# Strassen's block products for five of the eleven feature groups of each FFN, taken in turn with the down projections

## Chip, core and metric

One NeuronCore of one Trainium2 chip runs the whole program. The metric is the device time of one execution in microseconds (us). The kernel before takes 2244.43 us (median of three runs, 2243.63 to 2244.71).

## The reference

A causal decoder of two layers, 256 tokens, model width 2048, in float32. Both layers mix the tokens by attention and then run a gated MLP (the FFN). Layer 0 has dilated attention and four heads of attention to a memory of 256 tokens; layer 1 has stick-breaking attention and four memory heads. The change concerns the FFN alone:

```python
def _conv_ffn(h, w_up, w_conv, b_conv, w_down):
    u = h @ w_up                      # [256, 2048] @ [2048, 2 * 5632]
    gate, val = jnp.split(u, 2, axis=-1)
    gp = jnp.pad(gate, ((0, 0), (CONV_WIDTH - 1, 0), (0, 0)))
    acc = b_conv + gp[:, CONV_WIDTH - 1:CONV_WIDTH - 1 + S] * w_conv[CONV_WIDTH - 1]
    for j in range(CONV_WIDTH - 1):
        acc = acc + gp[:, j:j + S] * w_conv[j]
    return (jax.nn.silu(acc) * val) @ w_down      # [256, 5632] @ [5632, 2048]

def _finish_layer(x, heads, w_o, norms, ...):
    x = x + _rmsnorm(heads @ w_o, norms[1])
    f = _conv_ffn(_rmsnorm(x, norms[2]), ...)
    return x + _rmsnorm(f, norms[3])
```

## The kernel before

**Precision.** Every large product is made of float32r parts: each factor is split into an upper part, hi, and a rest, lo, and three of the four part products are summed (hi hi, lo hi, hi lo; `mm3`, L113 to L115). Weights come from HBM a megabyte at a time (`piece`): a load on the SP queue into one of three `raw` buffers, and then, for each half of 128x1024, a cast on ScalarE (L106, tile `whi`) and a subtraction on VectorE (L107, tile `wlo`); `whi` and `wlo` have four buffers each.

**Up projection.** Features are made in tiles of 128 (`ws_tile`). The weights stand in TensorE and h^T moves. For each of 16 k-tiles there is one matmul of 512 columns (hi of the weight against both parts of h^T, L129, the last one L132) and one of 256 (lo of the weight against hi of h^T, L130). One tile takes one megabyte of weights and 16 such pairs. ScalarE copies half of the PSUM bank out (L133) and VectorE adds the other half (L134). Two tiles make a pair (`ws_pair`): a gate pair, then its value pair. The gate pair is multiplied by 1/rms on VectorE (L576), convolved by one ScalarE instruction a tile (L581) and two VectorE instructions a tile (L584), passed through SiLU (L586), multiplied by 1/rms again (L592) and by the value pair (L595), and split into parts (L247 on ScalarE, L248 on VectorE).

**Down projection.** The activations stand and the weights move (`as_chunk`): a piece of 512 rows by 512 columns is 24 matmuls of 512 columns, into one PSUM bank for each of the two token tiles. PSUM has eight banks: four under the tag `g` and four under the tag `s`.

**Order.** `ffn` (L530 on) takes the 5632 features in parts of 4, 4, 4, 4, 4 and 2 pairs of tiles. After each part come its down projections, for four chunks of 512 columns: one piece a chunk for every 512 features. What they give is copied to the running sum `ys` (tag `sh`, SBUF) by ScalarE in the first part (L554) and added by VectorE in the others (L556). The Tile framework derives all waits and gives each engine its own instruction order from modelled costs; small steps of other work are hung at the start of later feature tiles (`later` and `step`). Layer 0's FFN lies at about 384 to 1134 us of the profiled execution, layer 1's at 1499 to 2226 us.

Of the kernel before, what the change touches and what calls it, by code (L numbers as in the profile page):

```python
# [29 lines left out]
# columns of the packed per-feature vectors  # L30
# [3 lines left out]
# FFN parts, in pairs of 128-feature tiles  # L34
PARTS = (4, 4, 4, 4, 4, 2)

# order in which the q and k tiles of mixer A are made: dilated head by head
# [6 lines left out]
class Body:  # L44
    def __init__(self, ctx, tc, a):
        self.tc, self.nc, self.a = tc, tc.nc, a
        self.sb = ctx.enter_context(tc.tile_pool(name="sb", bufs=1))
        self.todo = []
        self.psp = ctx.enter_context(tc.tile_pool(name="ps", bufs=1, space=bass.MemoryType.PSUM))

# [85 lines left out]
    def ws_pair(self, src, h, out=None, before=None, R=None):  # L136
        """Two of them, [P, 2, tok], times R."""
# [44 lines left out]
    def sums(self, n):  # L182
        """Room for the partial means of squares of n token tiles, with eps as the last part."""
# [4 lines left out]
    def rstd(self, ss):  # L188
        """[P, n, 5], the parts of mean(x^2) + eps -> 1 / rms, [P, n]."""
# [11 lines left out]
    def spread(self, r, name):  # L201
        """[P, 2] per token -> [P, 256], the same on every partition."""
# [15 lines left out]
    def scaled_T(self, src, kt, g, h):  # L218
        """h^T of one 128-feature tile, times its gain, in two parts."""
# [53 lines left out]
    def mem_heads(self, qm, mk, mv, outs, first):  # L273
        """Softmax attention to the memory, its steps taken at the coming units from `first` on."""
# [42 lines left out]
    def rotate(self, q, kinds):  # L317
        """Two feature tiles [e, 2, tok]: times 1 / rms and rotated (q also times E^-0.5)."""
# [77 lines left out]
    def sb_pair(self, j, q, k, V, outs, first):  # L396
        """Stick-breaking attention of heads 2j and 2j+1. q, k: [e, 2, tok]."""
# [5 lines left out]
    def sb_scores(self, q, k, st):  # L403
# [14 lines left out]
        # softplus(z), in the form that can't overflow  # L418
# [4 lines left out]
        # sums over this and the later keys  # L423
# [36 lines left out]
    def scaled_chunk(self, src, h, r, before=None, later=None):  # L460
        """[tok, 512] times r; `later`: r comes as late as that unit."""
# [15 lines left out]
    def add_normed(self, ys, r, t, each=None):  # L477
        """x += y g / rms(y) for one token tile; ys: four [tok, 2, 512] chunks that hold y g."""
# [8 lines left out]
    def out_proj(self, layer, src, lhs, each, filler=None):  # L487
# [3 lines left out]
        for c0 in (0, 2):  # L491
# [12 lines left out]
            # the first two chunks side by side: the last heads are needed late  # L504
# [11 lines left out]
            if late:  # L516
                # token tile by token tile: the end of the first one lies behind the second
# [12 lines left out]
    def ffn(self, layer, h, each, filler=None, done=None):  # L530
        nc = self.nc
        up, dn = self.a["up%d" % layer], self.a["dn%d" % layer]
# [6 lines left out]

        def spread():  # L540
# [3 lines left out]

        self.later(1, rms)
# [3 lines left out]
        base = 0  # L549

        def evac(part, c, t, b, gs):
            y = ys[c][:, t, :]
            if part == 0:
                nc.scalar.copy(y, b)  # L554
            else:
                nc.vector.tensor_add(y, y, b)  # L556
            if gs:
# [3 lines left out]
                nc.vector.tensor_tensor(y, y, gs[c], op=ALU.mult)  # L561

        for part, npairs in enumerate(PARTS):
            last = part == len(PARTS) - 1
            acts = []
            for p in range(base, base + npairs):
                if p % 2 == base % 2:
                    ahi = self.sh([P, 4, S], F32R)
                    alo = self.sh([P, 4, S], F32R)
                    o = 0  # L570
                ga = self.ws_pair(up[p, 0], h)
                if p == 0:
                    # 1 / rms of the first pair comes late
                    val = self.ws_pair(up[p, 1], h)
                Rb = spread().unsqueeze(1).to_broadcast([P, 2, S])
                nc.vector.tensor_tensor(ga, ga, Rb, op=ALU.mult)  # L576
                c = self.pairtile()
                for j in range(2):
                    ft = 2 * p + j
                    w = [self.cols[:, cv + i * NFT + ft:cv + i * NFT + ft + 1] for i in range(4)]  # L580
                    nc.scalar.activation(c[:, j, :], ga[:, j, :], AF.Identity, scale=w[2], bias=w[3])  # L581
                    for i in (1, 0):
                        d = 2 - i
                        nc.vector.scalar_tensor_tensor(c[:, j, d:], ga[:, j, :S - d], w[i], c[:, j, d:],  # L584
                                                       op0=ALU.mult, op1=ALU.add)
                nc.scalar.activation(c, c, AF.Silu)  # L586
                if layer == 0 and p == NFT // 2 - 1:
                    # one table set serves Exp and Ln in what follows
                    tc = self.tc
                    tc.keep_in_program_order(  # L590
                        nc.scalar.preload_act_table_set("natural_log_exp_and_others"))
                nc.vector.tensor_tensor(c, c, Rb, op=ALU.mult)  # L592
                if p:
                    val = self.ws_pair(up[p, 1], h)
                nc.vector.tensor_tensor(c, c, val, op=ALU.mult)  # L595
                self.split_heads(c, ahi[:, o:o + 2, :], alo[:, o:o + 2, :])
                acts += [(ahi[:, o + j, :], alo[:, o + j, :]) for j in range(2)]
                o += 2
# [261 lines left out]
```

## Time and profile before

| | |
|---|---|
| runs, median (lowest to highest) | 2244.43 us (2243.63 to 2244.71) |
| span of the profiled execution | 2242.5 us |
| TensorE (PE) busy | 2227.6 us, 99% |
| VectorE (DVE) busy | 1451.5 us, 65% |
| ScalarE (ACT) busy | 1148.6 us, 51% |
| GpSimd (POOL) busy | 19.0 us, 1% |
| granted TensorE clock, mean | 0.999 of full |
| moved by DMA | 422.39 MB, 188 GB/s |

PE, DVE, ACT, POOL and SP are the five engines. A busy time counts the execution of instructions and not the issue of transfers. A timeline row gives start, duration, engine, line, operation, destination<-sources, shape and count, and in brackets how long the engine had been idle and what ended that. Durations of successive instructions overlap a little, since an engine starts one before the last has drained: so the distance of two starts is the price of a queued instruction, and the duration that of one that stands alone.

### The profile page before, as it was taken

The numbers are of one execution on the slowest core, as the hardware profiler recorded it, in microseconds if no ns is written. First come the engines' busy times: TensorE is split into PE (matmuls) and PEld (weight loads), VectorE is DVE, ScalarE is ACT, GpSimd is POOL, SyncE is SP. The second block draws the span as 40 slices with busy tenths as digits, with TensorE's granted clock in tenths as the row PEclk, the third lists the DMA queues.
The fourth block names the chain that finished last, engine by engine and source line by source line (L and its number), as shares of the span: only waits on it lengthen the run. The fifth ranks groups of instructions, "written<-read, shape, count | busy, mean of one in ns | idle before, by whom it ended". The sixth has DMA issues, their size and how long they took to land.

```text
span 2242.5 us, 28970 instructions
## 1 busy us (share of the span) xinstructions
PE 2227.6 (99%) x11682; PEld 1895.7 (85%) x11682; DVE 1451.5 (65%) x1879; ACT 1148.6 (51%) x1614; POOL 19.0 (1%) x42
## 2 busy tenths in 40 slices
PE   9999999999999999999999999999999999999998
PEld 7888888888888888888888888878888888888886
DVE  6567767756656566665774676567566665666657
ACT  6545656545445454454564545455454454544544
POOL 0000000000000000000000000000000000000000
PEclk9999999999999999999999999999999999999999
DMA  8754555555555555555545445545555555555553
GB/s 309 269 180 160 191 194 182 188 188 188 188 188 188 188 188 188 188 188 189 187 169 188 154 166 179 190 176 188 188 188 188 188 188 188 188 188 188 188 188 131
DMA packets 61607, 422.39 MB, mean 188 GB/s; under 512 B 7073, under 2 KB 7457, under 8 KB 11937
## 3 DMA queue, kind: packets, MB, share of 16 engines
q1 hardware_dynamic: 60192, 416.35, 53.8%
q0 software_dynamic: 1280, 4.20, 0.7%
q8 instruction: 91, 1.49, 0.3%
q14 instruction: 44, 0.35, 0.0%
HBM read 418.42 MB, written 2.10 MB: 188 GB/s over the span
## 4 chain that ended last, share of the span: by engine, by line
PE 98%; issue 1%; DMA 0%; DVE 0%; ACT 0%; SPq 0%; POOLq 0%; POOL 0%; DVEq 0%; ACTq 0%
PE ps_g L129 38%; PE ps_g L130 20%; PE ps_g L113 12%; PE ps_g L115 11%; PE ps_g L114 11%; PE ps_g L132 3%; PE ps_s L234 1%; DMA raw<-in_wmv_dram 0%; PE ps_s L285 0%; PE ps_s L312 0%; PE ps_s L391 0%; PE ps_s L409 0%; PE ps_s L449 0%; PE ps_s L348 0%; PE ps_s L304 0%
## 5 line engine op out<-in xcount | busy, mean ns | idle before, releaser
L129 PE MATMUL ps_g<-h,whi 128*128 128x512 f32 x3600 | 1283.9, 399 | 0.2 <-DVE h L224 0.2
L107 DVE TENSOR_TENSOR wlo<-raw,whi 128x1024 fp32r<-128x1024 f32 (+1 forms) x758 | 924.3, 1221 | 534.6 <-ACT whi L106 531.3
L106 ACT CAST whi<-raw 128x1024 fp32r<-128x1024 f32 (+1 forms) x758 | 794.2, 1048 | 563.2 <-PE ps_g L114 341.2
L130 PE MATMUL ps_g<-h,wlo 128*128 128x256 f32 x3840 | 1038.5, 281 | 0.0
L129 PEld LDWEIGHTS ps_g<-h,whi 128*128 128x128 f32 x3600 | 676.2, 188 | 155.4 <-DVE h L224 0.7
L130 PEld LDWEIGHTS ps_g<-h,wlo 128*128 128x128 f32 x3840 | 724.8, 189 | 22.2
L113 PE MATMUL ps_g<-whi,sh 128*128 128x512 f32 x824 | 325.6, 395 | 0.0
L115 PE MATMUL ps_g<-wlo,sh 128*128 128x512 f32 x824 | 323.1, 392 | 0.0
L114 PE MATMUL ps_g<-whi,sh 128*128 128x512 f32 x824 | 320.4, 389 | 0.0
L133 ACT COPY qk<-ps_g 128x256 f32<-128x256 f32 x224 | 83.6, 373 | 337.5 <-PE ps_g L132 337.5
L134 DVE TENSOR_TENSOR qk<-ps_g,qk 128x256 f32<-128x256 f32 x224 | 95.0, 424 | 163.1 <-ACT qk L133 161.0
L115 PEld LDWEIGHTS ps_g<-wlo,sh 128*128 128x128 f32 x824 | 154.7, 188 | 36.0
L114 PEld LDWEIGHTS ps_g<-whi,sh 128*128 128x128 f32 x824 | 154.7, 188 | 34.4 <-DVE sh L248 0.3
L113 PEld LDWEIGHTS ps_g<-whi,sh 128*128 128x128 f32 x824 | 154.9, 188 | 30.8 <-ACT sh L247 0.2
L113 PE MATMUL ps_g<-whi,h 128*128 128x512 f32 x280 | 110.5, 395 | 2.0 <-ACT whi L106 2.0
L115 PE MATMUL ps_g<-wlo,h 128*128 128x512 f32 x280 | 109.7, 392 | 0.1
L114 PE MATMUL ps_g<-whi,h 128*128 128x512 f32 x280 | 109.6, 392 | 0.0
L132 PE MATMUL ps_g<-h,whi 128*128 128x512 f32 x240 | 95.6, 398 | 0.0
L584 DVE SCALAR_TENSOR_TENSOR qk<-qk,cols 128x254 f32<-128x254 f32 (+1 forms) x176 | 73.1, 478 | 0.0
L556 DVE TENSOR_TENSOR sh<-sh,ps_g 128x512 f32<-128x512 f32 x76 | 51.8, 684 | 21.5 <-PE ps_g L115 21.5
L113 PEld LDWEIGHTS ps_g<-whi,h 128*128 128x128 f32 x280 | 52.5, 188 | 14.5 <-ACT whi L106 3.6
L115 PEld LDWEIGHTS ps_g<-wlo,h 128*128 128x128 f32 x280 | 52.5, 188 | 12.9 <-DVE wlo L107 1.6
(152 smaller groups left out, 1059.7 us busy)
## 6 DMA issues: line engine op xcount, KB each, us to landing
raw<-in_up_dram SPq DMA_DIRECT2D x176, 1024.0 KB, 4.8
raw<-in_dn_dram SPq DMA_DIRECT2D x88, 1024.0 KB, 4.8
raw<-in_wqk_a_dram SPq DMA_DIRECT2D x24, 1024.0 KB, 4.9
raw<-in_wo_b_dram SPq DMA_DIRECT2D x16, 1024.0 KB, 4.9
raw<-in_wv_a_dram SPq DMA_DIRECT2D x12, 1024.0 KB, 4.8
raw<-in_wv_b_dram SPq DMA_DIRECT2D x12, 1024.0 KB, 4.8
raw<-in_wk_b_dram SPq DMA_DIRECT2D x12, 1024.0 KB, 4.8
raw<-in_wq_b_dram SPq DMA_DIRECT2D x12, 1024.0 KB, 4.8
```

The source lines that it names most:

```text
L106: nc.scalar.copy(hi[:, ns], r)
L107: nc.vector.tensor_sub(lo[:, ns], r, hi[:, ns].bitcast(F32))
L113: mm(out, lhi, rhi, start=start, stop=False)
L114: mm(out, llo, rhi, start=False, stop=False)
L115: mm(out, lhi, rlo, start=False, stop=stop)
L129: mm(b, whi[:, ks], both, start=kt == 0, stop=False)
L130: mm(b[:, 0:S], wlo[:, ks], one, start=False, stop=False)
L132: mm(b, whi[:, ks], both, start=False, stop=True)
L133: nc.scalar.copy(out, b[:, S:])
L134: nc.vector.tensor_add(out, b[:, 0:S], out)
L556: nc.vector.tensor_add(y, y, b)
L584: nc.vector.scalar_tensor_tensor(c[:, j, d:], ga[:, j, :S - d], w[i], c[:, j, d:], op0=ALU.mult, op1=ALU.add)
```

## The change

The features of one layer are seen as eleven groups of 512 gate and 512 value features. Groups 0, 2, 4, 6, 8 and 10 ("narrow") are made the old way. Groups 1, 3, 5, 7 and 9 ("wide") are made by a form of Strassen's scheme with seven block products and eight sums of results: token tile against token tile, k-tile against k-tile, gate against value. The new `wide` takes one group in eight units of two k-tiles. A unit is one megabyte of weights in four 128x512 blocks (b11, b21, b22, b12; array `uw`), from which VectorE makes the sums t1 and t3 and, in place, b22 and b21 (L584, L585, L588, L589); blocks and sums are split into parts (L573 on ScalarE, L574 on VectorE). Seven products of three matmuls of 512 columns each (L116 to L118) are summed over the units in seven PSUM banks. h^T stands; its own block sums are made once a layer (`sums_of_h`), in the place that memory's tile `h1` had. The parts `fc` and `fd` of a unit lie in one buffer, `forms`, in the place of the residual stream x, which is sent to DRAM (`xout`) early in the FFN and loaded again ahead of the last narrow group. At the end of a wide group two ScalarE instructions (L607) and eight VectorE ones (L610) make four [128 tokens, 512] tiles of the banks, with 1/rms applied; in `turned`, at the second and third tile of the next narrow group, sixteen PE transposes (L725) turn them, and convolution and product read them from PSUM.

Down projections are no longer taken after parts but in turn with the units: each wide group after a layer's first has eight units and eight down pieces (two groups by four chunks), and the first one has four. A token tile's half of a down piece has its own `s` bank, which ScalarE copies to an `sc` tile (L663; four buffers); an accumulating DMA issued by GpSimd adds that tile to `ys` (L664). There are 144 of these, each of 256 KB from SBUF to SBUF. Group 9's down pieces and group 10's stand at the end and are added as before. Layer 0 also makes the memory's h^T for layer 1 a second time, in its last narrow group (`again`, not shown).

```diff
+    def wide(self, src, h, s, forms, r):
+        ps = {i: self.bank("g" if i in (1, 2, 6, 7) else "s") for i in range(1, 8)}
...
+        for u in range(n):
+            raw = self.sb.tile([P, 2048], F32, name="raw", tag="raw", bufs=3)
+            nc.sync.dma_start(raw, src[u])
+            b11, b21, b22, b12 = (raw[:, i * 512:(i + 1) * 512] for i in range(4))
...
+            nc.vector.tensor_sub(t1, b12, b11)
+            nc.vector.tensor_sub(t3, b22, b12)
+            split(*fa, raw[:, 0:1024])
+            split(*(f[:, 0:512] for f in fb), b22)
+            nc.vector.tensor_sub(b22, b22, t1)
+            nc.vector.tensor_sub(b21, b21, b22)
+            for i, of in enumerate((t1, t3)):
+                split(*(f[:, i * 512:(i + 1) * 512] for f in fc), of)
+            split(*fd, raw[:, 512:1536])
+            product(1, u, *fa, 0)
+            product(2, u, *fa, 1)
+            product(3, u, *fb, 0)
+            yield
+            product(7, u, *fc, 1)
+            product(5, u, *fc, 0)
+            product(6, u, *fd, 1)
+            product(4, u, *fd, 0)
+            if u < n - 1:
+                yield
+        a = [self.sc([P, 512]) for _ in range(2)]
+        g0, v1 = self.sc([P, 512]), self.sc([P, 512])
...
+            nc.scalar.activation(a[t], ps[1], AF.Copy, scale=rt[t])
...
+        add(g0, 2, 0, a[0])
+        add(a[1], 7, 1, a[1])
...
-    def ffn(self, layer, h, each, filler=None, done=None):
+    def ffn(self, layer, h, each, filler=None, done=None, late=None):
...
+                part = self.sc([P, 512])
+                nc.scalar.copy(part, b)
+                nc.gpsimd.dma_start(y, part, accum_op=ALU.add)
+
+        def down(g, c):
+            parts = self.piece(dn[c, g])
+            for t in range(2):
+                b = self.bank("s")
+                self.as_mm([b, b], parts, acts[g], 0, (t,))
+                evac(g, c, t, b)
+                yield
...
+        narrow(0)
+        before, forms = [0], None
+        for g in WIDE:
...
+            w = self.wide(uw[WIDE.index(g)], h, s, forms, R[0])
+            downs = [down(b, c) for b in before for c in range(4)]
+            share = KT // 2 // len(downs)
+            for u in range(KT // 2):
+                d = downs[u // share] if u % share == 0 else iter(())
+                next(d, None)
+                next(w)
+                next(d, None)
+                next(w)
+            for i in range(2):
+                self.later(1 + i, lambda made=self.made, i=i, g=g: turned(g, made, i))
...
+            narrow(g + 1)
+            before = [g + 1, g]
```

In the orders below a row is one instruction: line, operation, destination<-sources with buffer numbers, shape. The first place is VectorE in the midst of an FFN. Before, between two up tiles:

```order
L584 SCALAR_TENSOR_TENSOR qk_5565<-qk_5473,cols_61,qk_5565 128x255 x2
L584 SCALAR_TENSOR_TENSOR qk_5565<-qk_5473,cols_61,qk_5565 128x254 x2
L107 TENSOR_TENSOR wlo_5673<-raw_5670,whi_5672 128x1024
L592 TENSOR_TENSOR qk_5565<-qk_5565,R_3509 128x512
L134 TENSOR_TENSOR qk_5574<-ps_g_5575,qk_5574 128x256
L107 TENSOR_TENSOR wlo_5677<-raw_5670,whi_5676 128x1024
L107 TENSOR_TENSOR wlo_5718<-raw_5715,whi_5717 128x1024
L134 TENSOR_TENSOR qk_5574<-ps_g_5620,qk_5574 128x256
L595 TENSOR_TENSOR qk_5565<-qk_5565,qk_5574 128x512
L107 TENSOR_TENSOR wlo_5722<-raw_5715,whi_5721 128x1024
L248 TENSOR_TENSOR sh_5472<-qk_5565,sh_5471 128x512
```

There the splitting of up weights (`wlo`) alternates with the convolution and with the sum of a tile's two bank halves. After, one unit of a wide group with its down piece:

```order
L584 TENSOR_TENSOR qk_5211<-raw_5209 128x512
L574 TENSOR_TENSOR x_3797<-raw_5124,x_3797 128x1024
L585 TENSOR_TENSOR qk_5212<-raw_5209 128x512
L110 TENSOR_TENSOR wlo_5186<-raw_5183,whi_5185 128x1024
L110 TENSOR_TENSOR wlo_5190<-raw_5183,whi_5189 128x1024
L574 TENSOR_TENSOR wlo_5214<-raw_5209,whi_5213 128x1024
L574 TENSOR_TENSOR wlo_5216<-raw_5209,whi_5215 128x512
L574 TENSOR_TENSOR x_3797<-qk_5212,x_3797 128x512
L588 TENSOR_TENSOR raw_5209<-raw_5209,qk_5211 128x512
L574 TENSOR_TENSOR x_3797<-qk_5211,x_3797 128x512
L589 TENSOR_TENSOR raw_5209<-raw_5209 128x512
```

The t1 of the next unit stands ahead of this unit's last split, and the two splits of the down piece (L110) ahead of the four of the unit's blocks. Nothing there reads PSUM any more.

The second place is PE between two up tiles. Before, the tile `ps_g_5866` ends and the next begins:

```order
L129 MATMUL ps_g_5866<-h2_2651,whi_5873 128x512
L130 MATMUL ps_g_5866<-h2_2651,wlo_5874 128x256
L129 MATMUL ps_g_5866<-h2_2651,whi_5873 128x512
L130 MATMUL ps_g_5866<-h2_2651,wlo_5874 128x256
L129 MATMUL ps_g_5866<-h2_2651,whi_5873 128x512
L130 MATMUL ps_g_5866<-h2_2651,wlo_5874 128x256 x2
L132 MATMUL ps_g_5866<-h2_2651,whi_5873 128x512
L129 MATMUL ps_g_5911<-h2_2651,whi_5914 128x512
L130 MATMUL ps_g_5911<-h2_2651,wlo_5915 128x256
L129 MATMUL ps_g_5911<-h2_2651,whi_5914 128x512
L130 MATMUL ps_g_5911<-h2_2651,wlo_5915 128x256
L129 MATMUL ps_g_5911<-h2_2651,whi_5914 128x512
```

After, the first up tile that follows a wide group, and what stands behind it:

```order
L132 MATMUL ps_g_5453<-h2_2654,whi_5460 128x512
L133 MATMUL ps_g_5453<-h2_2654,wlo_5461 128x256 x2
L135 MATMUL ps_g_5453<-h2_2654,whi_5460 128x512
L725 MATMUL ps_s_5499<-ident_65,sc_5440 128x128
L725 MATMUL ps_s_5499<-ident_65,sc_5439 128x128
L725 MATMUL ps_s_5499<-ident_65,sc_5440 128x128
L725 MATMUL ps_s_5499<-ident_65,sc_5439 128x128
L725 MATMUL ps_s_5504<-ident_65,sc_5438 128x128
L725 MATMUL ps_s_5504<-ident_65,sc_5441 128x128
L725 MATMUL ps_s_5504<-ident_65,sc_5438 128x128
L725 MATMUL ps_s_5504<-ident_65,sc_5441 128x128
L132 MATMUL ps_g_5498<-h2_2654,whi_5524 128x512
```

Eight transposes of the wide group's results (`sc`) stand between the first and the second up tile.

The third place is VectorE at the down projections' end. Before, the sums of down results, between splits:

```order
L107 TENSOR_TENSOR wlo_5404<-raw_5401,whi_5403 128x1024
L107 TENSOR_TENSOR wlo_5408<-raw_5401,whi_5407 128x1024
L556 TENSOR_TENSOR sh_3296<-sh_3296,ps_g_5327 128x512
L107 TENSOR_TENSOR wlo_5438<-raw_5435,whi_5437 128x1024
L556 TENSOR_TENSOR sh_3296<-sh_3296,ps_g_5328 128x512
L107 TENSOR_TENSOR wlo_5442<-raw_5435,whi_5441 128x1024
L107 TENSOR_TENSOR wlo_5478<-raw_5475,whi_5477 128x1024
L107 TENSOR_TENSOR wlo_5482<-raw_5475,whi_5481 128x1024
L556 TENSOR_TENSOR sh_3297<-sh_3297,ps_g_5399 128x512
L107 TENSOR_TENSOR wlo_5523<-raw_5520,whi_5522 128x1024
L556 TENSOR_TENSOR sh_3297<-sh_3297,ps_g_5400 128x512
```

After, the end of a wide group; the results of the down pieces have gone to the accumulating DMA, and the rows with `sc` are the eight sums of products:

```order
L110 TENSOR_TENSOR wlo_5525<-raw_5522,whi_5524 128x1024
L110 TENSOR_TENSOR wlo_5529<-raw_5522,whi_5528 128x1024
L610 SCALAR_TENSOR_TENSOR sc_5440<-ps_g_4778,small_3389,sc_5438 128x512
L610 SCALAR_TENSOR_TENSOR sc_5439<-ps_g_4783,small_3389,sc_5439 128x512
L610 SCALAR_TENSOR_TENSOR sc_5438<-ps_g_4782,small_3389,sc_5438 128x512
L610 SCALAR_TENSOR_TENSOR sc_5439<-ps_g_4782,small_3389,sc_5439 128x512
L610 SCALAR_TENSOR_TENSOR sc_5441<-ps_s_4781,small_3389,sc_5439 128x512
L610 SCALAR_TENSOR_TENSOR sc_5438<-ps_s_4781,small_3389,sc_5438 128x512
L610 SCALAR_TENSOR_TENSOR sc_5439<-ps_s_4780,small_3389,sc_5439 128x512
L610 SCALAR_TENSOR_TENSOR sc_5438<-ps_s_4779,small_3389,sc_5438 128x512
L110 TENSOR_TENSOR wlo_5602<-raw_5599,whi_5601 128x1024
L137 TENSOR_TENSOR qk_5452<-ps_g_5453,qk_5452 128x256
```

The eight sums stand behind four splits of up weights, of which the last two are shown; the PE rows above read their results.

More of the change, by code (lines that the diff above doesn't have):

```diff
@@ L538, in rms @@
             R.append(rx)
+            for t in range(2):
+                nc.sync.dma_start(self.xout[t], self.x[:, t, :])
         def spread():
@@ L543, in spread @@
             return R[1]
+        s, make = self.sums_of_h(h)
+        for i in range(KT // 2):
+            self.later(i, lambda i=i: make(i))
         self.later(1, rms)
@@ L561, in evac @@
                 nc.vector.tensor_tensor(y, y, gs[c], op=ALU.mult)
[L563 to L571, printed above, removed]
+            else:
+                part = self.sc([P, 512])
+                nc.scalar.copy(part, b)
+                nc.gpsimd.dma_start(y, part, accum_op=ALU.add)
@@ new lines, in ffn @@
+        for c in range(4):
+            g = WIDE[-1]
+            b = self.as_chunk(dn[c, g:], acts[g])
+            for t in range(2):
+                evac(g, c, t, b[t])
+        g = GROUPS - 1
+        gs = [self.gain(2 * layer + 1, c) for c in range(4)]
+        if not filler:
+            banks = [[self.bank(), self.bank()] for _ in range(2)]
+            banks += [[self.bank("s"), self.bank("s")] for _ in range(2)]
+            store = self.stores("h1") + self.stores("h2")
+            parts = [self.piece(dn[c, g], store=store[c]) for c in range(4)]
+            for t in range(2):
+                for c in range(4):
+                    self.as_mm(banks[c], parts[c], acts[g], 0, (t,))
+                    evac(g, c, t, banks[c][t], gs)
+                self.add_normed(ys, r[t], t, lambda c: done(t, c))
+            return
@@ L617, in ffn @@
+        for c in range(4):
+            b = self.as_chunk(dn[c, g:], acts[g])
+            for t in range(2):
+                evac(g, c, t, b[t], gs)
         self.add_normed(ys, r[0], 0)
```

161 lines of the change are left out of this document (115 added, 46 removed).

## The prediction

> **What bounds the kernel now.** I read the page's shares first, then its chain of waits, then one window inside layer 0's FFN.
>
> ```profile
> span 2242.5 us, 28970 instructions
> ...
> PE 2227.6 (99%) x11682; PEld 1895.7 (85%) x11682; DVE 1451.5 (65%) x1879; ACT 1148.6 (51%) x1614; POOL 19.0 (1%) x42
> ...
> PE 98%; issue 1%; DMA 0%; DVE 0%; ACT 0%; SPq 0%; POOLq 0%; POOL 0%; DVEq 0%; ACTq 0%
> ```
>
> The chain that ends last is TensorE for 98% of the span. The other engines and the transfers are covered, so only fewer or shorter matmuls shorten this kernel, as long as the cover lasts. How much cover there is stands in the windows (PE, PEld, DVE, ACT, POOL busy with counts, clock, share of the DMA engines, GB/s):
>
> ```profile
> 510.00:600.00 90.00, 90.00 (x508) 78.01 (x507) 59.76 (x77) 47.53 (x64) 0.00 (x0) 1.00 0.55 187
> ```
>
> VectorE has a third of its time free here, ScalarE half, the DMA engines 45%. At the granted clock of 1.00 the matmul paces come from two timelines. VectorE's, inside the up projections:
>
> ```profile
> 547.62 0.69 DVE L576 TENSOR_TENSOR qk<-qk,R 128x512 f32<-128x512 f32 x1
> 548.23 1.22 DVE L107 TENSOR_TENSOR wlo<-raw,whi 128x1024 fp32r<-128x1024 f32 x1
> 549.36 1.66 DVE L584 SCALAR_TENSOR_TENSOR qk<-qk,cols 128x255 f32<-128x255 f32 x4
> 550.94 1.22 DVE L107 TENSOR_TENSOR wlo<-raw,whi 128x1024 fp32r<-128x1024 f32 x1
> 552.07 0.69 DVE L592 TENSOR_TENSOR qk<-qk,R 128x512 f32<-128x512 f32 x1
> ...
> 558.46 0.42 DVE L134 TENSOR_TENSOR qk<-ps_g,qk 128x256 f32<-128x256 f32 x1 [1.05 <-ACT qk L133]
> 558.92 0.69 DVE L595 TENSOR_TENSOR qk<-qk 128x512 f32<-128x512 f32 x1
> 559.53 1.22 DVE L107 TENSOR_TENSOR wlo<-raw,whi 128x1024 fp32r<-128x1024 f32 x1
> 560.67 0.68 DVE L248 TENSOR_TENSOR sh<-qk,sh 128x512 fp32r<-128x512 f32 x1
> ...
> 569.77 0.42 DVE L134 TENSOR_TENSOR qk<-ps_g,qk 128x256 f32<-128x256 f32 x1 [1.01 <-ACT qk L133]
> ```
>
> L134 ends a feature tile. From 558.46 to 569.77 two tiles pass, so a tile costs (569.77 - 558.46) / 2 = 5.655 us of TensorE. The same rows price VectorE. Standing in a queue, a 128x1024 takes 560.67 - 559.53 = 1.14 us and a 128x512 takes 559.53 - 558.92 = 0.61; alone they take 1.22 and 0.69. TensorE's timeline in a down projection (L113 to L115 in turn):
>
> ```profile
> 497.62 0.39 PE L113 MATMUL ps_g<-whi,sh 128*128 128x512 f32 x1
> ...
> 501.05 0.39 PE L113 MATMUL ps_g<-whi,sh 128*128 128x512 f32 x1
> ```
>
> Fifteen matmuls lie between these two starts: 3.43 / 15 = 0.2288 us each, so a down piece of 24 costs 5.49.
>
> **TensorE's gain.** A group of 512 + 512 features is eight tiles: 8 x 5.655 = 45.2 us go. A wide group puts in their place 8 units x 7 products x 3 = 168 matmuls of the down projections' kind, 168 x 0.2288 = 38.4, and 16 transposes. Those are priced by a row of the chain:
>
> ```profile
> 368.87 1.75 PE ps_s L234 x16
> ```
>
> 16 cost 1.75 us. The net is 45.2 - 38.4 - 1.75 = 5.05 us a group, and 50.5 us for ten groups. All the rest of the sum is what the shorter cover lets through. The rows for that, groups of one form (count, busy, mean ns) and the transfers (median us from issue to landing):
>
> ```profile
> L107 DVE TENSOR_TENSOR wlo<-raw,whi 128x1024 fp32r<-128x1024 f32 x754 | 921.5, 1224 | 533.6 <-ACT whi L106 530.4 <-PE ps_s L234 1.6
> L106 ACT CAST whi<-raw 128x1024 fp32r<-128x1024 f32 x754 | 791.8, 1051 | 562.2 <-PE ps_g L114 341.2 <-PE ps_g L129 148.0 <-issue 59.3
> L224 DVE SCALAR_TENSOR_TENSOR h<-sh,cols,h 128x256 fp32r<-128x256 f32 x48 | 20.4, 481 | 5.4 <-ACT h L223 5.4
> L247 ACT CAST sh<-qk 128x512 fp32r<-128x512 f32 x44 | 27.4, 622 | 12.0 <-DVE qk L595 12.0
> L554 ACT COPY sh<-ps_g 128x512 f32<-128x512 f32 x16 | 9.3, 582 | 15.3 <-PE ps_g L115 15.3
> L483 DVE SCALAR_TENSOR_TENSOR x<-sh,small,x 128x512 f32<-128x512 f32 x32 | 22.3, 750 | 1.2 <-POOL small L194 0.9
> L474 POOL DMA_DIRECT2D sc<-in_gb_dram x16 | 9.0, 560 | 559.3 <-DVE sc L440 252.3 <-DVE qk L134 199.1 <-DVE sh L500 68.2
> ```
>
> ```profile
> raw<-in_up_dram SPq DMA_DIRECT2D x176, 1024.0 KB, 4.8
> ...
> sc<-in_gb_dram POOLq DMA_DIRECT2D x16, 256.0 KB, 4.5
> ...
> x<-in_x_dram SPq DMA_DIRECT2D x2, 1024.0 KB, 6.8
> ```
>
> **A unit with its down piece.** TensorE needs 21 + 24 matmuls, 45 x 0.2288 = 10.30 us. VectorE needs seven 128x512 (t1, t3, b22, b21, fb, two halves of fc) and two 128x1024 (fa, fd), 7 x 0.61 + 2 x 1.14 = 6.55, and 2.28 for the piece: 8.83 queued, 7 x 0.69 + 4 x 1.22 = 9.7 alone. Both lie under 10.30, but only by 15 and 6%. ScalarE has four casts of 1024, three of 512 and two bank copies, 4 x 1.05 + 3 x 0.62 + 2 x 0.58 = 7.2. TensorE still leads. An order of these instructions walked by hand with those durations has VectorE finish each form 4 to 5 us before TensorE wants it, and each `s` bank is copied out 1.3 us before its next use: no stall from these.
>
> **Loads.** By VectorE's order a unit's load can start when the second split of a piece (L110) has freed a `raw` buffer; it must have landed for that unit's t1; and behind t1 come the last unit's fd, t3 and the next piece's two splits, 2 x 0.61 + 3 x 1.14 = 4.64, with 0.08 for the last to drain. So a loop of load, sums, splits and release closes in L + 4.72 us, L being a load's landing. It costs TensorE nothing while that is under 10.3 us, L under 5.6; beyond, 8 x (L - 5.58) builds up over a group, of which the 4.4 us of VectorE's lead are free. L was 4.8 with the loads evenly spaced. In the new order a piece's load and a unit's start 3.7 us apart, so the second shares the engines with the first for 4.8 - 3.7 = 1.1 us, and the 0.5 MB of accumulation add to it. From the window: 90 us at 0.55 and 187 GB/s move 16.8 MB, so a megabyte takes 3.1 us of all 16 engines and 256 KB takes 0.77. Half of a 0.77 lands on such a load: L = 4.8 + 1.1 + 0.35 = 6.25. That is 8 x 0.67 - 4.4 = 1.0 us a group, 8 us for the eight groups of this kind. The ends are 0 (L = 4.8) and, with the x loads' 6.8, 5.4 a group.
>
> **End of a wide group.** The eight sums wait for four splits of up weights, and the fifth (into `v1`) waits for an `sc` buffer that the last accumulating DMA must have read and released. That tile is copied out 4.3 us after the last units' start (S); with the 4.5 us of the 256 KB row, `v1` starts at about S + 9 and the sums that follow take three times 0.7. TensorE meets the first transposes behind one tile, at S + 5.5 + 5.65 = S + 11.15. So the stall is 0 to 1.8; I take 1.0, times eight: 8 us. Behind it wait up tiles on TensorE and their splits on VectorE. Each microsecond by which the accumulation lands later is a microsecond here. The Trainium skill's page DMA: Bandwidth & Descriptors (Anatomy of one DMA — SWDGE (gpsimd) path) gives about 2.0 us plus bytes / 436 GB/s for a transfer issued by GpSimd, an estimated 2.6 us here; by it the 8 us would vanish, but the row of this trace has 4.5, and the sum goes by the row.
>
> **The first wide group of a layer** has four pieces for eight units: TensorE 8 x 4.80 + 4 x 5.49 = 60.4 us, VectorE 8 x 6.55 + 4 x 2.28 = 61.5. VectorE is the bound there, and its splits start up to 4.1 us behind the end of group 0, since the last product and split of that group stand ahead of them: 1.1 + 4.1 = 5.2 a layer, 10.4 in all. With durations taken alone VectorE would have 8 x 7.27 + 4 x 2.44 = 68.
>
> **The narrow groups.** VectorE has 16 splits, eight L134, conv and products, and the turned halves: about 42 us queued, 47.5 alone, against 8 x 5.655 + 1.75 = 47.0. No stall, or 0.5. In group 0 no sums of products or turned halves stand, but eight makings of h^T's block sums do: 2 x 0.61 and four of 128 elements, each at most the 0.42 of an L134, so 1.2 to 2.9 us; at 2.0 that group needs 45 against 45.2, and I take 1 us a layer. The memory's h^T made again is 16 x 0.48 = 8 us of VectorE in the last narrow group, for which I take 2, and 0.5 a layer for a later start of the FFN: 5 in all. x to DRAM and back hides under 700 us. The 144 accumulations keep GpSimd at 144 x 0.56 = 81 us of a span of 2242; it has nothing else.
>
> **The sum:** -50.5 + 8 + 8 + 10.4 + 5 = -19.1. From the span 2242.5 - 19.1 = 2223.4; the median lies 1.9 above the span, so 2225.
>
> **Rivals.**
> All covers hold: loads stay near 4.8 and the accumulation lands sooner than VectorE gets to `v1`. What is left is half of the first groups' 10.4 and the 5: -50.5 + 10 = -40, 2204. For it speak the free shares in the window, against it that the first group has no cover left on VectorE.
>
> VectorE takes over, with instructions that cost what they cost alone, since most of the new ones wait for a cast: first groups 2 x (68 - 60.4 + 4.1) = 23, ends 8 x 1.8 = 14, narrow groups 8 x 0.5 = 4 and group 0 2 x 3 = 6, the memory 3: +50, and nothing is gained, 2244. For it speaks that VectorE stood 530 us idle before L107 for L106; against it that L106 itself stood idle for TensorE (341 and 148 us), which frees the buffers, and not for its own speed.
>
> Slower: the accumulating DMAs fill the 16 engines. Each reads its tile, and reads and writes `ys`. At 6.8 us a load, as for x beside other loads, a group loses 5.4 us, 43 for eight: -50.5 + 43 + 23.4 = +16, 2261; at 7.0 it would be 2274. The point from which the change loses is L = 6.54, only 0.3 above what I take. For it speaks the short margin; against it that the bytes rise by a tenth and the engines are at 0.55. The Trainium skill's page DMA: Bandwidth & Descriptors (Issuing engines are not separate DMA queues) says that transfers of all issuing engines run on the same 16 engines and interleave; by that the loads do pay for the accumulation, which is this rival. The 6.8 agrees with it.
>
> That the change doesn't do what it says I leave at nothing: the order has 1680 matmuls of 512 more and 1280 pairs fewer.
>
> **How the numbers follow.** A measurement tells about 0.2%, 4.5 us, from no change. My sum has 0.48, the covers 0.17, VectorE 0.14, the accumulation 0.21. Of the first a little reaches into the zone of no change, and a little of VectorE's out of it. Faster 0.64, same 0.14, slower 0.22. The range goes from 2206, just above where all covers hold, to 2258, just under the slower rival's 2261; alone, my own case would have 2212 to 2238.
>
> **What would show it.** In the profile after: TensorE's share down from 99% by the stalls (about 31 us of idle time), PE waits on `sc` at L725 of about 1 us, on the forms at L116 in the first wide group of each layer, the megabyte of `uw` landing in about 6.3 us. I am wrong if those loads land under 5.5 (then it is faster) or over 6.5, if VectorE's 512-wide rows stand at 0.69 apart, or if the transposes wait more than 2 us.

## The result and the profile after

The changed kernel takes 2327.75 us (median of four runs, 2317.21 to 2337.0) against 2244.03: the ratio is 1.037, 95% interval 1.035 to 1.039. It is slower by 84 us where 19 less were forecast, and outside the range.

The page of the changed kernel, with its transfers (section 6: KB each, median us from issue to landing):

```profile
span 2329.3 us, 29420 instructions
...
PE 2221.3 (95%) x10962; PEld 1845.9 (79%) x10962; DVE 1760.9 (76%) x2447; ACT 1328.2 (57%) x1970; POOL 142.0 (6%) x186
...
q0 software_dynamic: 22016, 41.95, 9.9%
...
PE 48%; issue 41%; POOL 5%; DVE 3%; DMA 2%; ACT 1%; SPq 0%; POOLq 0%; DVEq 0%; ACTq 0%
...
raw<-in_uw_dram SPq DMA_DIRECT2D x80, 1024.0 KB, 6.7
sh<-sc POOLq DMA_DIRECT2D x144, 256.0 KB, 7.0
```

Of the 144 accumulating DMAs 128 stand in the wide groups with eight pieces, 16 in each, and the other 16 carry group 9's down pieces at the layers' ends; only group 10's are added as before.

TensorE has 720 matmuls fewer and 108 us without work, where before it had 15. The chain doesn't tell why: 41% of it is "issue", time that it puts down to nothing. So I read stages. In TensorE's records a wide group with eight pieces runs from its first L116 to the first L132 behind it: the eight of them took 88.6 to 92.5 us, mean 91.0, against 82.4 of matmuls. The narrow group behind it took 52.3 to 54.5 us against 47.0 (without the one that also makes the memory's h^T). The same two stages in windows (columns as in the prediction), one wide group and the narrow one behind it:

```profile
681.00:773.00 92.00, 85.91 (x364) 68.23 (x362) 71.75 (x89) 54.84 (x75) 13.48 (x16) 0.98 0.76 217
773.00:828.00 55.00, 49.88 (x276) 43.07 (x274) 41.29 (x61) 26.89 (x41) 0.10 (x1) 0.94 0.53 176
```

VectorE is busy for 72 of 92 us: it isn't the bound, though TensorE waits. The DMA engines went from 0.55 to 0.76. What was waited for (us in total, times, longest), over the whole span:

```profile
DVE qk L584 <- DMA raw<-in_uw_dram: 119.1, 49, 4.0
...
PE ps_s L116 <- ACT sc L663: 46.3, 42, 2.1
DVE sc L610 <- issue: 42.2, 15, 4.3
...
PE ps_s L725 <- DVE sc L610: 35.5, 8, 5.1
```

There are two stalls. **In the wide group** VectorE's t1 (L584) waits for the unit's load, and TensorE waits for ScalarE's copy of an `s` bank (L663). The queue of SP and VectorE's timeline show how they hang together:

```profile
714.92 0.33 SPq L578 DMA_DIRECT2D raw<-in_uw_dram  x1
...
725.89 0.33 SPq L578 DMA_DIRECT2D raw<-in_uw_dram  x1
...
738.70 0.33 SPq L578 DMA_DIRECT2D raw<-in_uw_dram  x1
...
749.86 0.33 SPq L578 DMA_DIRECT2D raw<-in_uw_dram  x1
```

```profile
712.54 2.36 DVE L110 TENSOR_TENSOR wlo<-raw,whi 128x1024 fp32r<-128x1024 f32 x2
...
722.30 0.69 DVE L584 TENSOR_TENSOR qk<-raw 128x512 f32<-128x512 f32 x1 [0.84 <-DMA raw<-in_uw_dram]
...
723.51 2.36 DVE L110 TENSOR_TENSOR wlo<-raw,whi 128x1024 fp32r<-128x1024 f32 x2
...
733.98 0.69 DVE L584 TENSOR_TENSOR qk<-raw 128x512 f32<-128x512 f32 x1 [3.97 <-DMA raw<-in_uw_dram]
```

A piece's second split ends at 712.54 + 2.36 = 714.90, and the load starts at 714.92; t1 starts at 722.30, 7.4 us later; the next two splits end at 725.87, and the next load starts at 725.89. It is the loop of the prediction, closing in 11.0, 12.8 and 11.2 us where TensorE needs 10.30. From t1 to the release of the buffer it takes 4.7 us, as predicted, or 3.6, as from 722.30, where fd's split has gone ahead of t1.

How this reaches TensorE is in ScalarE's row order. The cast of fd waits for VectorE's L589, the copy of the `s` bank stands behind that cast, and TensorE waits for the copy:

```profile
719.16 1.04 ACT L573 CAST x<-raw 128x1024 fp32r<-128x1024 f32 x1 [5.82 <-DVE raw L589]
720.11 0.58 ACT L663 COPY sc<-ps_s 128x512 f32<-128x512 f32 x1
```

```profile
720.74 0.50 PE L116 MATMUL ps_s<-whi,sh 128*128 128x512 f32 x1 [2.03 <-ACT sc L663]
```

**Behind the wide group** TensorE's timeline shows the first transposes:

```profile
778.83 0.27 PE L725 MATMUL ps_s<-ident,sc 128*128 128x128 f32 x1
784.23 1.77 PE L725 MATMUL ps_s<-ident,sc 128*128 128x128 f32 x7 [5.12 <-DVE sc L610]
```

and VectorE's and GpSimd's the reason:

```profile
775.09 2.73 DVE L610 SCALAR_TENSOR_TENSOR sc<-ps_g,small,sc 128x512 f32<-128x512 f32 x4 [1.94 <-issue]
782.10 2.73 DVE L610 SCALAR_TENSOR_TENSOR sc<-ps_s,small,sc 128x512 f32<-128x512 f32 x4 [4.28 <-issue]
```

```profile
767.83 0.85 POOL L664 DMA_DIRECT2D sh<-sc  x1 [7.07 <-ACT sc L663]
772.26 0.84 POOL L664 DMA_DIRECT2D sh<-sc  x1 [3.58 <-ACT sc L663]
```

The first four sums start 7.3 us after the last accumulating DMA but one was issued, the second four (`v1` first) 9.8 us after the last one. That one landed just before them. The transfers issued between 772.0 and 772.5 are this one:

```profile
sh<-sc POOLq DMA_DIRECT2D x1, 256.0 KB, 9.8
```

In all eight groups the last one took 8.5 to 9.8 us to land, and the second four sums started within 0.1 us of it. The wait itself bears no name, "issue"; that it is the `sc` buffers had to be tested.

### The profile page after: what moved, and what is told of

It reads as the page before. It is cut to its first block, busy times and chain, and to the rows that moved or that the text cites. A ratio compares the mean times of both kernels' runs of the same rounds, so it can differ in the third digit from the quotient of the medians.

```text
span 2329.3 us, 29420 instructions
## 1 busy us (share of the span) xinstructions
PE 2221.3 (95%) x10962; PEld 1845.9 (79%) x10962; DVE 1760.9 (76%) x2447; ACT 1328.2 (57%) x1970; POOL 142.0 (6%) x186
## 4 chain that ended last, share of the span: by engine, by line
PE 48%; issue 41%; POOL 5%; DVE 3%; DMA 2%; ACT 1%; SPq 0%; POOLq 0%; DVEq 0%; ACTq 0%
PE ps_g L132 16%; PE ps_g L133 9%; PE ps_g L116 5%; PE ps_g L118 5%; PE ps_g L117 5%; POOL sh L664 4%; PE ps_g L135 1%; PE ps_s L116 1%; PE ps_s L118 1%; PE ps_s L117 1%; DMA sh<-sc 1%; DVE wlo L110 1%; PE ps_s L237 1%; DMA sc<-in_gb_dram 0%; DVE x L574 0%
## 5 line engine op out<-in xcount | busy, mean ns | idle before, releaser
L110 DVE TENSOR_TENSOR wlo<-raw,whi 128x1024 fp32r<-128x1024 f32 (+1 forms) x598 | 720.4, 1219 | 225.9 <-ACT whi L109 222.3
L132 PE MATMUL ps_g<-h,whi 128*128 128x512 f32 x2400 | 868.6, 403 | 0.9 <-ACT whi L109 0.7
L133 PE MATMUL ps_g<-h,wlo 128*128 128x256 f32 x2560 | 696.7, 282 | 1.6 <-DVE wlo L110 1.6
L132 PEld LDWEIGHTS ps_g<-h,whi 128*128 128x128 f32 x2400 | 456.9, 190 | 107.1 <-ACT sc L607 1.8
L133 PEld LDWEIGHTS ps_g<-h,wlo 128*128 128x128 f32 x2560 | 489.0, 191 | 15.2 <-DVE wlo L110 2.8
L116 PE MATMUL ps_s<-whi,sh 128*128 128x512 f32 x576 | 232.9, 405 | 46.7 <-ACT sc L663 46.3
L573 ACT CAST x<-raw 128x1024 fp32r<-128x1024 f32 x80 | 83.9, 1049 | 260.5 <-DVE raw L589 207.4
L118 PE MATMUL ps_s<-wlo,sh 128*128 128x512 f32 x576 | 228.7, 397 | 0.0
L117 PE MATMUL ps_s<-whi,sh 128*128 128x512 f32 x576 | 227.4, 395 | 1.0 <-DVE sh L251 1.0
L664 POOL DMA_DIRECT2D sh<-sc x144 | 122.5, 851 | 1372.5 <-ACT sc L663 1358.8
L116 PEld LDWEIGHTS ps_s<-whi,sh 128*128 128x128 f32 x576 | 109.4, 190 | 90.2 <-ACT sc L663 67.0
L116 PE MATMUL ps_g<-whi,h 128*128 128x512 f32 x440 | 172.7, 392 | 1.9 <-ACT whi L109 1.8
L117 PE MATMUL ps_g<-whi,h 128*128 128x512 f32 x440 | 172.3, 392 | 0.0
L118 PE MATMUL ps_g<-wlo,h 128*128 128x512 f32 x440 | 171.0, 393 | 0.1
L136 ACT COPY qk<-ps_g 128x256 f32<-128x256 f32 x144 | 53.5, 371 | 177.0 <-PE ps_g L135 176.8
L573 ACT CAST whi<-raw 128x1024 fp32r<-128x1024 f32 (+1 forms) x160 | 131.0, 836 | 40.0 <-DMA raw<-in_uw_dram 15.4
L574 DVE TENSOR_TENSOR wlo<-raw,whi 128x1024 fp32r<-128x1024 f32 (+1 forms) x160 | 146.8, 956 | 0.0
L584 DVE TENSOR_TENSOR qk<-raw 128x512 f32<-128x512 f32 x80 | 55.4, 693 | 119.1 <-DMA raw<-in_uw_dram 119.1
L117 PEld LDWEIGHTS ps_s<-whi,sh 128*128 128x128 f32 x576 | 109.3, 190 | 25.7 <-DVE sh L251 3.0
L118 PEld LDWEIGHTS ps_s<-wlo,sh 128*128 128x128 f32 x576 | 109.3, 190 | 24.5
L574 DVE TENSOR_TENSOR x<-raw,x 128x1024 fp32r<-128x1024 f32 x80 | 97.9, 1224 | 30.6 <-ACT x L573 30.5
```

The lines of the kernel that those rows point to most:

```text
L110: nc.vector.tensor_sub(lo[:, ns], r, hi[:, ns].bitcast(F32))
L116: mm(out, lhi, rhi, start=start, stop=False)
L117: mm(out, llo, rhi, start=False, stop=False)
L118: mm(out, lhi, rlo, start=False, stop=stop)
L132: mm(b, whi[:, ks], both, start=kt == 0, stop=False)
L133: mm(b[:, 0:S], wlo[:, ks], one, start=False, stop=False)
```

## The experiments

Theory A: the accumulating DMAs are the whole loss, through these two waits. They make the unit loads land later, and they hold the `sc` buffers. Theory B: the loads are late by VectorE's, ScalarE's and the raw buffers' order, and the DMAs only hold `sc`. Each run is compared with the kernel before on the same chip; stage lengths are read as above.

**e1, no accumulating DMA**

```diff
                 nc.scalar.copy(part, b)
-                nc.gpsimd.dma_start(y, part, accum_op=ALU.add)
```

> The 144 accumulating DMAs are left out (the bank copies to sc stay), so the sums of the down products are missing. Theory A, the accumulating DMAs are the cause: they delay the unit loads (6.7 us landing) and they hold the sc buffers that the eight sums need. Without them the unit load lands in about 5.2 us, the loop of 5.2 + 4.7 fits into 10.3, a wide group with eight pieces falls from 91 to about 83 us, and the stall at the transposes goes: 2329 - 68 - 50, about 2212. Theory B, the loads are late by the order of VectorE and ScalarE and of the raw buffers, and the accumulating DMAs only hold sc: loads stay at 6.5, wide groups at 90, the ends alone gain: about 2275.

2212.58 us, ratio 0.986 (0.984 to 0.988). Its unit loads:

```profile
raw<-in_uw_dram SPq DMA_DIRECT2D x80, 1024.0 KB, 4.9
```

A window over one of its wide groups:

```profile
538.00:620.70 82.70, 82.70 (x361) 67.28 (x360) 72.32 (x90) 56.33 (x75) 0.00 (x0) 1.00 0.59 203
```

The order of all other instructions is that of the changed kernel. Wide groups take 82.7 us, narrow ones 46.9, and TensorE's idle time there is gone. Theory B is refuted: in the same order the loads come back to 4.9 by themselves. The bank copies are in time again too: in the later units of a group the copy behind fd's cast ends 1.29 us before TensorE's next use of the bank, where in the changed kernel it ends 0.05 us before.

**e3, VectorE adds**

```diff
-                part = self.sc([P, 512])
-                nc.scalar.copy(part, b)
-                nc.gpsimd.dma_start(y, part, accum_op=ALU.add)
+                nc.vector.tensor_add(y, y, b)
```

> Down results are added to the running sum by VectorE from PSUM, as before the change; no copy, no DMA. VectorE has 8.83 + 1.22 = 10.05 us a unit against TensorE's 10.30. Theory A: unit loads land in about 5.2, the loop has at most one more add in it (5.2 + 4.7 + 0.6 = 10.5), the ends don't stall: 2215 to 2230, faster than before. Theory B: VectorE at 97% of the unit stays late, no gain against the changed kernel but at the ends: 2270 or more.

2211.17 us (2209.29 to 2213.28), ratio 0.985 (0.984 to 0.987): the whole computation, 1.5% under the kernel before. One of its wide groups, and its unit loads:

```profile
663.09:745.76 82.67, 82.67 (x362) 67.42 (x361) 79.70 (x105) 46.76 (x59) 0.00 (x0) 1.00 0.53 192
```

```profile
raw<-in_uw_dram SPq DMA_DIRECT2D x80, 1024.0 KB, 6.6
```

VectorE is busy for 79.7 of 82.7 us, 96%, and TensorE doesn't wait. The time was a little under what I gave, but the loads landed in 6.6 us and not in about 5.2. In this run's order a piece's load and a unit's start 1.1 us apart, so without any accumulating DMA they are nearly as late as in the changed kernel. They cost nothing here, because this order lets them start early enough: a late landing is a loss only where t1 and the bank copy wait for it.

**e4, GpSimd adds**

```diff
-                nc.gpsimd.dma_start(y, part, accum_op=ALU.add)
+                nc.gpsimd.tensor_add(y, y, part)
```

> The accumulating DMA is replaced by an addition on GpSimd (sc to the running sum, 128x512, both in SBUF). Theory A: as without the DMAs, 2212 to 2225, if GpSimd takes under 4 us an addition and VectorE's rows keep their 0.61 apart; if VectorE's rows get longer beside GpSimd, up to 2260. Theory B: 2275.

2296.73 us, ratio 1.023 (1.022 to 1.025), more than either theory gave. Unit loads land in 4.8 us, yet wide groups take 92. The groups of e4 show the reason, where the same three VectorE rows of the changed kernel have 1223, 689 and 693 ns. Below them is one of its wide groups:

```profile
L664 POOL TENSOR_TENSOR sh<-sh,sc 128x512 f32<-128x512 f32 x144 | 302.5, 2104 | 1160.7 <-ACT sc L663 1160.6
L574 DVE TENSOR_TENSOR wlo<-raw,whi 128x1024 fp32r<-128x1024 f32 x80 | 131.3, 1641 | 0.0
...
L585 DVE TENSOR_TENSOR qk<-raw 128x512 f32<-128x512 f32 x80 | 83.3, 1042 | 0.0
...
L584 DVE TENSOR_TENSOR qk<-raw 128x512 f32<-128x512 f32 x80 | 73.5, 919 | 4.8 <-DMA raw<-in_uw_dram 4.6
```

```profile
675.21:767.08 91.87, 85.79 (x362) 68.07 (x360) 85.64 (x89) 55.09 (x75) 33.77 (x16) 0.98 0.53 179
```

VectorE is busy for 85.64 us of this group, 10.7 a unit, which is more than TensorE's 10.30.

One meeting, in the timelines of the two engines:

```profile
714.31 1.85 POOL L664 TENSOR_TENSOR sh<-sh,sc 128x512 f32<-128x512 f32 x1 [4.68 <-ACT sc L663]
```

```profile
714.92 1.79 DVE L584 TENSOR_TENSOR qk<-raw 128x512 f32<-128x512 f32 x1
```

GpSimd ran until 716.16, and the L584 whose turn came at 714.92 ended at 716.71: 0.55 us, nearly its own duration, behind GpSimd. The Trainium skill's page SBUF — State Buffer (Who interferes with whom) has it so: a VectorE instruction with two SBUF inputs and a GpSimd one that reads SBUF share a port, and the later waits to the end of the first. The trace agrees.

**e5, two results outside `sc`**

```diff
-        g0, v1 = self.sc([P, 512]), self.sc([P, 512])
+        g0, v1 = (self.sb.tile([P, 512], F32, name="qk", tag="qk", bufs=5) for _ in range(2))
```

> Two of the four results of a wide group (g0 and v1) lie in buffers of the tag qk in place of sc, so the eight sums no longer wait for the last two accumulating DMAs. The order of all instructions is unchanged. If these waits make the stall at the transposes (5.7 us, and 1.5 in the tile behind it, per group): 2328 - 8 x 7.2, about 2270, wide groups still 91 us. If VectorE's order makes it: above 2315.

2272.4 us (2266.02 to 2278.07), ratio 1.013 (1.010 to 1.016), as expected. Narrow groups take 46.9 us, wide ones still 87 to 91, and in its list of waits L725 is missing. The wait called "issue" was for the `sc` buffers.

**e2, the same transfers without accumulation**

```diff
-                nc.gpsimd.dma_start(y, part, accum_op=ALU.add)
+                nc.gpsimd.dma_start(y, part)
```

> The 144 transfers stay, of the same size and from the same queue, but they copy and don't accumulate (the down sums are thereby not formed). If it is the accumulation itself, reading ys and adding, that costs: the transfer lands in about 5 us in place of 7.0, the unit loads in about 5.5, and the time falls to about 2235. If it is any 256 KB from GpSimd's queue in rows of 2 KB: landing stays near 7, time 2300 or more.

2229.74 us, ratio 0.994 (0.992 to 0.996). Its queue of GpSimd's transfers, their issue and landing:

```profile
q0 software_dynamic: 12800, 41.95, 5.4%
...
L664 POOL DMA_DIRECT2D sh<-sc x144 | 77.4, 537 | 1324.1 <-ACT sc L663 1317.6
...
raw<-in_uw_dram SPq DMA_DIRECT2D x80, 1024.0 KB, 5.3
sh<-sc POOLq DMA_DIRECT2D x144, 256.0 KB, 4.0
```

Accumulating is most of the cost. For the same bytes it lands in 7.0 us and not 4.0, takes 0.85 us of GpSimd and not 0.54, and, without the 1280 packets and 0.7% that the queue had before, 20736 packets and 9.2% of 16 engines against 11520 and 4.7%: 0.092 x 2329 / 144 = 1.49 us of all engines each against 0.73. The plain copies aren't free: e2 is 17 us above e1, of the 115 us between e1 and the changed kernel.

**e6, the bank copies on VectorE**

```diff
-                nc.scalar.copy(part, b)
+                nc.vector.tensor_copy(part, b)
```

> All accumulating DMAs stay; only the copy from the bank to sc moves from ScalarE to VectorE (10.05 us a unit). With that the order puts the two splits of a piece ahead of t1 of the next unit, so a raw buffer is free almost a whole unit before its load is needed. Theory of the load loop: loads may land in 6.7 and more without a stall, wide groups fall from 91 to 83 to 86 us, the ends keep their 7 us: 2328 - 8 x 6, about 2275. Rival, ScalarE's order holds the bank copies: the same sign, but then the wait for the unit loads on VectorE (119 us in all) would stay; by the load loop it goes. If the accumulating DMAs slow TensorE in another way: wide groups stay at 90.

2247.84 us, ratio 1.001 (1.000 to 1.003), lower than expected. Wide groups take 82.7 us, the narrow ones 50.8 to 53.9, and the last one 46.8. The unit loads now land in 7.6 us, later than in the changed kernel, and t1's wait for them, 119 us there, is gone. In this run's trace the wait at the end of the wide groups also has a name, the accumulating DMA:

```profile
DVE sc L610 <- DMA sh<-sc: 25.5, 7, 4.7
...
DVE qk L584 <- DMA raw<-in_uw_dram: 0.6, 1, 0.6
```

Its queue and VectorE's timeline show why the loads no longer matter:

```profile
711.66 0.33 SPq L578 DMA_DIRECT2D raw<-in_uw_dram  x1
```

```profile
722.48 0.68 DVE L584 TENSOR_TENSOR qk<-raw 128x512 f32<-128x512 f32 x1
```

The load of 711.66 is wanted at 722.48, 10.8 us later. In the changed kernel t1 waits for it. The run takes the bank copies out of ScalarE's order as well, so it doesn't tell what either would do alone.

**e7, raw buffers divided**

```diff
-        raw = self.sb.tile([P, 2048], F32, name="raw", tag="raw", bufs=3)
+        raw = self.sb.tile([P, 2048], F32, name="raw", tag=tag, bufs=2 if tag == "raw" else 1)
...
-            parts = self.piece(dn[c, g])
+            parts = self.piece(dn[c, g], tag="rawd")
```

> The three raw buffers are divided: two for up weights and units, one for the down pieces taken in turn. All else stays, accumulating DMAs too. A unit's buffer is then free after its own fd split and not after the next piece's, 3.7 us earlier; a load has about 7.9 us. Theory of the load loop: wide groups with eight pieces fall from 91 to about 83 us though a unit load still takes 6 to 7 us, the ends keep their stall of 7: 2328 - 8 x 8, about 2264. Rival, ScalarE's order or VectorE itself is late: wide groups stay at 90, time above 2310.

2283.31 us, ratio 1.017 (1.013 to 1.020): two thirds of the gain expected. In one wide group the unit loads are waited for once and no more six times; in its place stands the load of the down piece, which has one buffer now:

```profile
ACT whi L109 <- DMA raw<-in_dn_dram: 8.5, 5, 2.6
...
DVE qk L584 <- DMA raw<-in_uw_dram: 2.2, 1, 2.2
```

Wide groups took 84 to 91 us; the first ones of each layer became longer, 67 to 69 for 63. The edit moved the loop to another buffer. **e8** is e7 with e5's edit:

> e7 with the buffers of e5: the accumulating DMAs stay, and both places where something waits for them or their neighbours are bought off by buffers. If the two stalls are all that the change lost: near the run without accumulating DMAs, 2210 to 2216, faster than before the change. If the traffic costs more than its two waits: 2230 or more.

2261.54 us, ratio 1.009 (1.007 to 1.012): the ends went, the loop through the down piece stayed. By the expectation this would mean a cost beyond the two waits, but one of the two, now at the down piece's load, had not been bought off; so it doesn't decide.

**e9, e6 and e5 together** tests it cleanly.

> e6 (bank copies on VectorE, whose order gives the unit loads almost a whole unit) with the buffers of e5 (g0 and v1 outside sc). All 144 accumulating DMAs stay. If the change lost its time in the two waits alone, both are gone: wide groups 82.7 us, narrow ones 46.9, near the run without the DMAs, 2208 to 2214. If the DMAs cost something beside the two waits: 2225 or more.

2212.56 us (2211.78 to 2216.26), ratio 0.986 (0.985 to 0.988). All 144 accumulating DMAs run, and the time is that of e1, which has none. A wide group of it:

```profile
666.10:748.80 82.70, 82.70 (x361) 67.39 (x360) 79.74 (x104) 46.95 (x59) 13.51 (x16) 1.00 0.85 238
```

The DMA engines are at 0.85, fuller than in the changed kernel (0.76), the unit loads land in 7.6 us, and TensorE doesn't wait. So it was the two waits, not the bandwidth.

**e10, e3 with the first wide group's products ahead of the down piece**

```diff
+                if share == 2:
+                    next(w)
                 next(d, None)
-                next(w)
+                if share == 1:
+                    next(w)
```

> e3 (VectorE adds, no accumulating DMA), and in the first wide group of a layer the first three products of a unit come ahead of the down piece and not behind its first half, so that TensorE has work while the activations of group 0 are still being split. The first wide group took 63.5 us against 60.4 of matmuls. If that lateness is what costs: 1 to 3 us less a layer, 2206 to 2210. If VectorE's work (61.5 us) bounds that group: 2211, as e3.

2212.33 us, ratio 0.986 (0.984 to 0.987): no gain on e3. The first wide groups took 66 to 67 us for 63, and the narrow ones behind them 47.1 for 49.2: work only moved between the two. By the expectation that speaks for VectorE as the bound, and so does its busy time in the changed kernel's first wide group, 62.4 of 63.4 us:

```profile
422.64:486.01 63.37, 61.15 (x260) 47.94 (x259) 62.38 (x87) 42.63 (x60) 0.00 (x0) 1.00 0.51 183
```

No run takes work from VectorE there, so that bound isn't shown.

## Why the prediction was wrong

**TensorE's gain was right.** Without the two stalls (e1, e3, e9) a wide group takes 82.7 us where 82.4 was worked out, a narrow one 46.7 to 46.9 where 47.0 was. The scheme is worth what the matmul count says.

**VectorE's terms were right in size.** The first wide groups took 63.4 and 63.7 us against 60.4, and the narrow ones behind them 49.3 and 49.1 against 47.0: 5.3 a layer for 5.2. Six matmuls of the last unit, 1.4 us, run behind the first up tile's start and so count with the narrow group; most of the loss is in the wide one, as predicted. Its cause, VectorE, is likely but not shown (e10). The rival "VectorE takes over" did not happen: its queued instructions kept to 0.61 and 1.14, and e3 ran with VectorE at 96% of a wide group.

**The load loop is the first step that failed**, in two of its terms. The loop itself was right: with a load's median it closes in 6.7 + 4.72 = 11.4 us, and 11.0 to 12.8 were read above.

The first term is the load's landing. L was 6.7 and not 6.25, and that these lie so near is luck. In e1 the order is the same and a unit's load starts 3.6 us behind a piece's (median), yet it lands in 4.9: of the 1.1 us given to sharing with the piece's load next to nothing is there. The accumulating DMAs, put at 0.35, added 1.8. In the third to eighth loads of a group, where both are in flight, it is more: 7.5 in the median against e1's 4.9. The 0.35 came from a price of 0.77 us of all engines, that of a load. For a plain copy it would have done: in e2, at 0.73, the loads land in 5.3. An accumulating one takes 1.49, twice as much, and delays the loads over four times as much; why it is more than twice no run shows.

The second is "4.4 us of VectorE's lead are free". That lead was counted at the forms. The copy of an `s` bank stands behind fd in ScalarE's row order, as shown above, and had only 1.3 us to spare, as the prediction itself says some lines earlier and e1 measures (1.29). So lateness reached TensorE almost at once. With the prediction's sum, L = 6.7 alone would have given 8 x (6.7 - 5.58) - 4.4 = 4.6 us a group, a lead of 1.3 alone 8 x 0.67 - 1.3 = 4.1, both together 7.7. Measured were 91.0 - 82.7 = 8.3, and the seven steps from one unit load to the next in a group add up to 82.0 us against e1's 73.6, 8.4 more. In place of 8 us, 66.

**The end of the group is the second.** The landing of the accumulating DMA was taken from a 256 KB load, 4.5 us; it was 7.0 in the median and 8.5 to 9.8 at the place that counts. The stall is 4.4 us in the mean (35.5 / 8), up to 5.1, and not 1.0, and it has an echo: the clock falls, below. By the narrow groups it is 6.7 each: their mean of 53.5 less the 46.8 that they take without it. In place of 8 us, about 54. The path was the predicted one; the landing was mis-sized.

**The account.** With the two measured terms the sum is -50.5 + 66 + 54 + 10.4 + 5 = +85; the spans differ by 2329.3 - 2242.5 = 86.8. Without the two stalls it is -50.5 + 10.4 + 5 = -35; e1's span is 31.7 us under that of before. Two of the prediction's signs of being wrong came true: loads over 6.5 and transposes that wait more than 2 us. The slower rival named the right cause, a load's landing beyond 6.54. Its price, 2261, was too small for the same two reasons: the free lead, and the ends left at their 8 us. The chance of 0.22 hung on the nearness of 6.25 to 6.54. The first number hung on the price of a transfer that no row of before showed, the second on the lead of 4.4.

The Trainium skill's fit (DMA: Bandwidth & Descriptors, Anatomy of one DMA — SWDGE (gpsimd) path), 2.6 us for such a transfer, was further off than the row: a plain copy of that size landed in 4.0 us in e2, an accumulating one in 7.0.

## What to carry to other kernels

A lead is only as long as the shortest one among all that must be ready; count it at every operand and bank that the bounding engine waits for, and along the row order of each engine on the way. Price a transfer of a new kind (accumulating, SBUF to SBUF) at twice the nearest plain one or more until it has been measured, and look at what holds its source buffer. Where buffers are few, an addition on an engine with free time in that stage (e3) can do as well as a transfer that leaves the engine free (e9), and it holds no buffer.

## What the runs showed of the hardware

After the pause of 5.12 us ahead of the transposes, TensorE ran at half pace for a while. Four of its records:

```profile
786.44 0.63 PE L132 MATMUL ps_g<-h,whi 128*128 128x512 f32 x1
...
789.00 0.63 PE L132 MATMUL ps_g<-h,whi 128*128 128x512 f32 x1
...
789.59 0.40 PE L132 MATMUL ps_g<-h,whi 128*128 128x512 f32 x1
...
792.39 0.39 PE L132 MATMUL ps_g<-h,whi 128*128 128x512 f32 x1
```

Between the first two lie four pairs of L132 and L133, 0.64 us each; between the last two eight, 0.35 each. The granted clock (last but two of the columns) in two windows:

```profile
784.20:789.40 5.20, 5.17 (x18) 4.46 (x19) 4.53 (x7) 1.13 (x2) 0.00 (x0) 0.50 0.17 32
789.40:793.00 3.60, 3.60 (x22) 3.20 (x21) 2.03 (x4) 1.58 (x2) 0.00 (x0) 0.98 0.59 246
```

A stall of 5.1 us thus cost some 2.5 us more: the seven transposes left took 785.65 - 784.23 = 1.42 us for 0.7, and the tile behind them 793.08 - 785.65 = 7.43 for 5.65.

A shorter pause can do it too. Behind the one of 2.03 us at 720.74, in the wide group, the granted clock was at half for 3.4 us and the matmuls stood 0.43 us apart for 0.23:

```profile
721.26:724.67 3.41, 3.41 (x9) 2.66 (x9) 2.57 (x5) 2.36 (x3) 0.57 (x1) 0.50 0.55 140
```

The 0.98 of that group's window is this stretch. Two other wide groups had one, behind pauses of 1.95 and 1.86 us; each costs up to 1.7 us, a part of the 8.3. One of 2.14 us, ended at 1046.20, was followed by none, so the pause's length alone doesn't settle it.

The Trainium skill's page TensorE: Matmul & The Clock Gate (What's actually happening) has TensorE fall to half its clock after about 3.4 us of idleness and return after about as long under load. The pause of 5.12 us agrees with the fall, those of about 2 us don't. The return took about 5.2 us of work behind the long pause and 3.9 behind the one of 2.03 (720.74 to 724.67).
